# Gated attention's output product and the last pair of MLP groups by seven block products each

## The chip, the cores and the metric

The kernel runs on one core of one Trainium2 chip, as one program. The metric is the device time of one execution in microseconds. A core has a matrix engine (TensorE, PE, with its weight loader PEld), three engines for elementwise work (VectorE or DVE, ScalarE or ACT, GpSimd or POOL), a queue processor that issues the DMAs (SyncE, SP), an on-chip memory (SBUF) and eight banks of 128x512 fp32 in which matmuls accumulate (PSUM).

## The reference

A trunk of two layers on one sequence of 512 tokens with 1024 features. Layer 0 mixes tokens by gated linear attention, layer 1 by stick-breaking attention on keys and values that are projected once. Behind each mixer and each MLP stands a LayerNorm of `ALPHA * h + y`. Cut to the parts that the change touches:

```python
def gla_mixer(x, w_in, w_a2, b_a, norm_g, w_o):
    ...
    o = o * lax.rsqrt(jnp.mean(jnp.square(o), axis=-1, keepdims=True) + RMS_EPS)
    o = o * norm_g.astype(jnp.float32)
    o = o * jax.nn.silu(g.astype(jnp.float32).reshape(B, S, GLA_HEADS, GLA_HEAD_V))
    return o.reshape(B, S, GLA_V).astype(x.dtype) @ w_o

def sq_relu_mlp(x, w_up, w_down):
    h = jax.nn.relu(x @ w_up)
    return (h * h) @ w_down

def reference(...):
    for layer in range(DEPTH):
        ...
        h = layer_norm(DEEPNORM_ALPHA * h + mix, ln_g[layer, 0], ln_b[layer, 0])
        h = layer_norm(DEEPNORM_ALPHA * h + sq_relu_mlp(h, mlp_w_up[layer], mlp_w_down[layer]),
                       ln_g[layer, 1], ln_b[layer, 1])
    return h
```

`gla_w_o` is 1024x1024, `mlp_w_up` 1024x4096, `mlp_w_down` 4096x1024, all fp32.

## The kernel before

**Arithmetic.** fp32 operands are split into a high and a low half in the format fp32r: ScalarE writes `hi` (a copy with rounding), VectorE writes `lo = raw - hi`. A product of two split tiles is three matmuls, hi x hi, hi x lo and lo x hi (`mm3`, L91 to L95). One tile step is 128 tokens, 128 of the contraction and 512 output columns.

**Tiles.** Tokens are four tiles of 128. The residual rows are the four tiles `h` of 128x1024 (class `Rows`): `add` puts a finished PSUM bank into one half of a row (L165 or L167), `stat` takes its statistics (L175), `stats` makes mean and variance from both halves (L179, L181) and on GpSimd the power -1/2 (L183), `centre` subtracts and scales (L187), `affine` applies gain and bias in four pieces of 512 columns (L193). Activations that serve as the stationary or contracted side are kept feature-major in tiles `T` of 128x4x512; PE makes them from rows by 128x128 transposes. `turn_affine` transposes four blocks of a row (L211), applies gain and bias on ScalarE while leaving PSUM (L214) and splits the result (`put`, L98 and L99).

**Weights** come by DMA in pieces of 128x1024 (two contraction tiles of 512 columns, or eight of 128), through 3 buffers `raw`, and are split into 6 buffers each of `hi` and `lo` (L70, L72).

**Gated attention, last part.** For each half n of the 1024 features and each token tile t, `gate` makes the gate product, its Silu and the gated row `os_`; `turn_gated` transposes four blocks of it into `onT`, a split operand. The output product takes `onT` with `gla_w_o`: first the columns 0 to 511 of all four token tiles, 24 matmuls for each, then the columns 512 to 1023 tile by tile inside `finish`. `finish` calls for each tile t: the product of the tile, its `stats`, its `centre`, and then the transposes of tile t-1 (`turn`). So tile t-1 is turned on PE behind the product of tile t. The transposes of the last tile are returned as `late` and run in the middle of the next stage.

**MLP.** Its 4096 hidden features are eight groups of 512. `up(g)` makes a group's product (96 matmuls), then relu (L543, ScalarE) and square (L544, VectorE) into a tile `s2` (three buffers). The groups are taken down in pairs. The pairs (0,1), (2,3) and (4,5) go through `down`: with hidden tokens and weights as 2x2 blocks (256 tokens, a group of 512, 512 columns) it makes the pair's 2x2 result by seven block products instead of eight, each of 24 matmuls of 512 columns (L592), 168 in all. Its operands are sums and differences of the blocks, made on VectorE, of activations (`s1`, `s2`, in place of `a21` and `a12`) and of weights (in place in the 8 buffers `B`), and each is split before use. A bank collects several products; its state is added to a row after each of them. The pair (6,7) goes through `down_last`: 192 matmuls by `mm3`, for columns 0 to 511 first group by group, then for columns 512 to 1023 tile by tile, in layer 0 inside `finish` as above, in layer 1 inside a loop which applies the last norm to each row and sends it out (`norm`, L198 to L204). There the last tile goes in two halves of 256 columns (L649).

**Order.** Each engine runs its own list of instructions in order; the order between engines comes from semaphores on the tiles. The program's text, a scheduler that moves instructions within it, and the number of buffers in each pool set the lists. SyncE issues all weight DMAs in the order of the text as their buffers come free.

## Time and profile before

| | |
|---|---|
| median of 3 runs | 1151.99 us (1151.84 to 1152.28) |
| the profiled execution's own time | 1152.1 us |
| its span | 1150.4 us |
| granted clock of TensorE, mean | 0.998 |
| matmuls with weight load on PE | 5485 |

The span is what the profiler saw from the first to the last instruction; the rest of the profiled execution's time lies around it. In the profile a row of the timeline or of the chain is start and duration in us, engine, line, operation, out<-in by the names of the program, shapes; what is in square brackets is the idle time of the engine ahead of it and what ended that. A window's row is its bounds, its length, busy time and number of instructions of PE, PEld, DVE, ACT and POOL, the granted clock, the DMA engines' busy share and GB/s. Each digit of part 2 below is a fortieth of the span:

```profile
PE   8999999999999999999999999999999999999997
DVE  4576644786877857845834878786958868678556
ACT  4454433543534524623634666654534435346320
```

The gated output product lies at 181.5 to 228 us, the MLP of layer 0 at 235 to 566, its last pair from 520 us on, and the last pair of layer 1 from 1099.4 us to the end.

### The profile page before, as it was taken

What the parts mean: (1) busy time and instruction counts of PE and PEld (TensorE: products, weight loads), DVE (VectorE), ACT (ScalarE), POOL (GpSimd) and SP (SyncE); (2) the same over time, 40 slices, a digit from 0 to 9 for tenths busy, and PEclk for the clock granted to TensorE, in tenths of its full rate; (3) what the DMA queues carried; (4) which work ended last, traced back from release to release, by engine and by line L of the source; (5) the groups of instructions that cost most, each with busy time, mean ns of one, the idle gap of its engine ahead of it and who ended that gap; (6) DMA issues with size and microseconds to landing.
All of it is one profiled execution on the core that took longest, in us unless ns stands there. A gap on an engine that the chain in (4) does not pass through costs nothing.

```text
span 1150.4 us, 14083 instructions
## 1 busy us (share of the span) xinstructions
PE 1133.6 (99%) x5485; PEld 939.9 (82%) x5485; DVE 795.9 (69%) x984; ACT 513.9 (45%) x784; POOL 96.5 (8%) x159
## 2 busy tenths in 40 slices
PE   8999999999999999999999999999999999999997
PEld 6788888898888888888888877778988888888886
DVE  4576644786877857845834878786958868678556
ACT  4454433543534524623634666654534435346320
POOL 1010100000000000000101444340000000000001
PEclk9999999999999999999999999999999999999999
DMA  7441123292360450142244111111732613601402
GB/s 234 125 122 45 53 89 132 79 284 78 110 198 22 148 167 15 37 148 93 72 128 126 58 56 56 57 54 37 248 119 86 203 42 112 198 20 37 135 31 74
DMA packets 86214, 118.71 MB, mean 103 GB/s; under 512 B 11202, under 2 KB 36930, under 8 KB 86148
## 3 DMA queue, kind: packets, MB, share of 16 engines
q1 hardware_dynamic: 86148, 117.81, 32.4%
q8 instruction: 43, 0.70, 0.2%
q14 instruction: 23, 0.19, 0.1%
HBM read 115.70 MB, written 2.10 MB: 102 GB/s over the span
## 4 chain that ended last, share of the span: by engine, by line
PE 83%; DVE 11%; ACT 2%; issue 2%; POOL 1%; DMA 0%; SPq 0%; DVEq 0%; POOLq 0%; ACTq 0%
PE ps L93 20%; PE ps L592 20%; PE ps L94 20%; PE ps L95 20%; DVE r L754 4%; DVE lo L72 2%; ACT wt L769 1%; DVE h L193 1%; DVE ps L746 1%; DVE T L99 1%; DVE qs L729 1%; ACT hi L70 1%; PE ps L121 1%; DVE bst L175 1%; POOL rs L183 1%
## 5 line engine op out<-in xcount | busy, mean ns | idle before, releaser
L72 DVE TENSOR_TENSOR lo<-raw,hi 128x1024 fp32r<-128x1024 f32 x152 | 185.3, 1226 | 156.2 <-ACT hi L70 154.3
L93 PE MATMUL ps<-T,hi 128*128 128x512 f32 (+1 forms) x768 | 288.7, 376 | 0.0
L95 PE MATMUL ps<-T,lo 128*128 128x512 f32 (+1 forms) x768 | 285.5, 372 | 0.0
L94 PE MATMUL ps<-T,hi 128*128 128x512 f32 (+1 forms) x768 | 285.5, 372 | 0.0
L70 ACT ACTIVATE hi<-raw 128x1024 fp32r<-128x1024 f32 x152 | 161.7, 1067 | 238.0 <-PE ps L94 109.5
L592 PE MATMUL ps<-hi,T 128*128 128x512 f32 x672 | 207.9, 389 | 0.0
L93 PE MATMUL ps<-hi,T 128*128 128x512 f32 (+1 forms) x456 | 179.2, 393 | 0.0
L95 PE MATMUL ps<-hi,T 128*128 128x512 f32 (+1 forms) x456 | 176.8, 388 | 0.0
L94 PE MATMUL ps<-lo,T 128*128 128x512 f32 (+1 forms) x456 | 176.6, 387 | 0.0
L95 PEld LDWEIGHTS ps<-T,lo 128*128 128x128 f32 x768 | 144.7, 188 | 25.1
L93 PEld LDWEIGHTS ps<-T,hi 128*128 128x128 f32 x768 | 144.7, 188 | 24.6 <-issue 1.1
L94 PEld LDWEIGHTS ps<-T,hi 128*128 128x128 f32 x768 | 144.8, 189 | 23.4
L592 PEld LDWEIGHTS ps<-hi,T 128*128 128x128 f32 x672 | 126.1, 188 | 26.3
L592 PE MATMUL ps<-lo,T 128*128 128x512 f32 x336 | 130.7, 389 | 0.0
L70 ACT ACTIVATE hi<-B 128x1024 fp32r<-128x1024 f32 x72 | 76.3, 1059 | 109.3 <-PE ps L94 75.3
L72 DVE TENSOR_TENSOR lo<-B,hi 128x1024 fp32r<-128x1024 f32 x72 | 87.5, 1222 | 46.2 <-ACT hi L70 45.8
L95 PEld LDWEIGHTS ps<-hi,T 128*128 128x128 f32 x456 | 85.9, 188 | 17.7 <-DVE T L99 0.3
L93 PEld LDWEIGHTS ps<-hi,T 128*128 128x128 f32 x456 | 86.1, 189 | 17.4 <-issue 1.3
L94 PEld LDWEIGHTS ps<-lo,T 128*128 128x128 f32 x456 | 86.0, 189 | 16.7 <-DVE lo L99 0.3
L183 POOL TENSOR_TENSOR rs<-ve,mhalf 128x1 f32<-128x1 f32 x16 | 12.8, 800 | 784.2 <-DVE ve L181 784.2
L167 DVE TENSOR_TENSOR h<-ps,h 128x512 f32<-128x512 f32 x91 | 62.4, 686 | 20.7 <-PE ps L95 20.5
L592 PEld LDWEIGHTS ps<-lo,T 128*128 128x128 f32 x336 | 63.1, 188 | 12.9
(155 smaller groups left out, 1168.8 us busy)
## 6 DMA issues: line engine op xcount, KB each, us to landing
raw<-in_mlp_w_up_dram SPq DMA_DIRECT2D x64, 512.0 KB, 4.0
B<-in_mlp_w_down_dram SPq DMA_DIRECT2D x48, 512.0 KB, 4.4
raw<-in_mlp_w_down_dram SPq DMA_DIRECT2D x28, 512.0 KB, 3.7
raw<-in_gla_w_in_dram SPq DMA_DIRECT2D x20, 512.0 KB, 3.9
raw<-in_kv_w_dram SPq DMA_DIRECT2D x16, 512.0 KB, 4.1
raw<-in_gla_w_o_dram SPq DMA_DIRECT2D x8, 512.0 KB, 5.1
raw<-in_sb_w_q_dram SPq DMA_DIRECT2D x8, 512.0 KB, 3.8
raw<-in_sb_w_o_dram SPq DMA_DIRECT2D x8, 512.0 KB, 3.6
```

What stands on the lines that cost most here:

```text
L70: nc.scalar.activation(hi, raw, AF.Copy)
L72: nc.vector.tensor_tensor(lo, raw, hi.bitcast(F32), op=ALU.subtract)
L93: nc.tensor.matmul(ps, lhsT=a[0], rhs=b[0], start=first, stop=False)
L94: nc.tensor.matmul(ps, lhsT=a[0], rhs=b[1], start=False, stop=False)
L95: nc.tensor.matmul(ps, lhsT=a[1], rhs=b[0], start=False, stop=last)
L99: keep(nc.vector.tensor_tensor(lo, ps, hi.bitcast(F32), op=ALU.subtract))
L121: nc.tensor.transpose(out=ps[:, 128 * i:128 * i + 128], in_=src[:, 128 * i:128 * i + 128], identity=ident)
L167: nc.vector.tensor_tensor(h, ps, h, op=ALU.add)
L175: nc.vector.bn_stats(out=self.st[:, parts * n + i, :], in_=h)
L183: nc.gpsimd.tensor_tensor(rs, ve, mhalf[:, 0:1], op=ALU.pow)
L592: nc.tensor.matmul(banks[s], lhsT=a(k, s)[x], rhs=b[k][y], start=opens and (k, x, y) == (0, 0, 0), stop=closes and (k, x, y) == (3, 1, 0), ...
L754: nc.vector.tensor_tensor_scan(down, down, begins[kind][:, ::-1], 1.0, op0=ALU.mult, op1=ALU.max)
```

## The change

`down` becomes a generator `seven` outside of the MLP, which takes the two halves of an activation (each 128x4x512 fp32), a function that gives the weight blocks, a pool for the buffers `B`, and the rows. It makes the same seven block products in another order, and adds to a row after each:

- a11 with block b(2), a12 with b(3), s2 with b(2), s1 with b(1): as before, 24 matmuls each for two token tiles;
- a12 (now changed) with the plain block, first for token tile 0, then for token tile 1, with a `yield` behind each: these rows are complete;
- for token tile 2 the products of a21 with b(0) and of a22 with b(3), a `yield`, then both for token tile 3.

The middle pairs run it to its end. The last pair is passed to `finish` (layer 0) or to the loop of the last norm (layer 1), which takes one step for each token tile; `down_last` and `parts` go. In layer 1 (`narrow`) the very last product goes in two halves of 256 columns. The gated output product goes through `seven` too. For that, `turn_gated` writes `onT` as plain fp32 by one copy on ScalarE (L594) in place of a split; the last of these transposes runs behind the first product (`mid`), and the sums s1 and s2 behind it. The pool `heads` is closed earlier, and a pool `gated` with 4 buffers `sg` and 8 buffers `B` stands in its place. `Rows.st`, the tile of a row's statistics, is made at the first `stat`, whichever half comes first.

The core of the diff (the body of `down` that goes is the body of `seven` that is kept, but for the order):

```diff
+    def seven(a1, a2, weights, pool, hs, fresh, norms=False, mid=None, narrow=False):
...
+        def raw(h, k, j):
+            b = pool.tile([P, 1024], F32, tag="B", bufs=8, name=nm("B"))
+            nc.sync.dma_start(out=b.rearrange("p (a b) -> p a b", a=2), in_=weights(k, h, j))
+            return b
...
+            for c in pieces:
+                for k in range(4):
+                    for x, y in ((0, 0), (0, 1), (1, 0)):
+                        nc.tensor.matmul(banks[s][:, c], lhsT=a(k, s)[x], rhs=b[k][y][:, c],
+                                         start=opens and (k, x, y) == (0, 0, 0),
+                                         stop=closes and (k, x, y) == (3, 1, 0), skip_group_check=True)
...
+        if not mid:
+            sums()
+        for b22, b12, b11, b21 in bs:
+            tt(b22, b22, b12, op=ALU.subtract)
+            tt(b12, b12, b11, op=ALU.subtract)
+        product(split_a(a11), split_b(2), ys, True, False, 0, 0)
+        if mid:
+            mid()
+            sums()
+        q12 = split_a(a12)
+        tt(a21, a11, a21, op=ALU.subtract)
+        product(q12, split_b(3), xs, True, True, 0, 0, last=True)
+        tt(a12, a12, s2, op=ALU.subtract)
+        for b22, b12, b11, b21 in bs:
+            tt(b11, b22, b11, op=ALU.add)
+            tt(b21, b21, b11, op=ALU.subtract)
+        product(split_a(s2), split_b(2), ys, False, False, 0, 1)
+        product(split_a(s1), split_b(1), zs, True, False, 1, 1)
+        how = split_a(a12), plain_b(1, 1), zs, False, True, 0, 1
+        for s in range(2):
+            part(s, *how, last=True)
+            yield
+        hows = [(split_a(a21), split_b(0), ys, False, False, 1, 1), (split_a(a22), split_b(3), ys, False, True, 1, 0)]
+        for s in range(2):
+            for how in hows:
+                part(s, *how, last=True)
+            yield
...
-        transpose_into(onT, n, t, os_[t][:, 512 * n:512 * n + 512])
+        ps = bank()
+        for i in range(4):
...
+        nc.scalar.activation(onT[n][:, :, 128 * t:128 * t + 128], ps.rearrange("p (a b) -> p a b", a=4), AF.Copy)
...
-    pcs = pieces_512(gla_w_o[0], 0, 8, 0)
-    for t in range(NT):
-        hs[t].add(0, rows(onT, t, pcs, K8), True, True)
-        if t == 0:
-            turn_gated(3, 1)
+    steps = seven(*onT, lambda k, h, j: block(gla_w_o[0], 512 * k + 256 * h, 512 * j), opp, hs, True, norms=True,
+                  mid=lambda: turn_gated(3, 1))
     hT = Split()
-    pcs = pieces_512(gla_w_o[0], 0, 8, 512)
-    late = finish(lambda t: hs[t].add(1, rows(onT, t, pcs, K8), True, True), vcols, hs, hT, g2)
+    late = finish(lambda t: next(steps), vcols, hs, hT, sgs)
...
-        sqs = [parts(sq[NG - 2]), parts(up(NG - 1))]
-        got = down_last(NG - 2, *sqs)
+        steps = down(NG - 2, norms=True, narrow=l == 1)
+        got = done(lambda t: next(steps), work)
```

**How the lists of the engines move: the start of layer 0's last pair.** ScalarE in the kernel before, around the relu of the last group (L543, tile s2673); T655 is the high half of group 6's activations (s2602), which the first matmuls of the pair take, and each `hi` a piece of weights:

```order
L98 ACTIVATE T655_3968<-s2602_3661 128x512 x4
L70 ACTIVATE hi658_3980<-raw657_3978 128x1024
L70 ACTIVATE hi661_3986<-raw660_3984 128x1024
L70 ACTIVATE hi664_3992<-raw663_3990 128x1024
L70 ACTIVATE hi667_3998<-raw666_3996 128x1024
L70 ACTIVATE hi677_4123<-raw676_4121 128x1024
L70 ACTIVATE hi680_4129<-raw679_4127 128x1024
L70 ACTIVATE hi683_4135<-raw682_4133 128x1024
L70 ACTIVATE hi686_4141<-raw685_4139 128x1024
L70 ACTIVATE hi697_4259<-raw696_4257 128x1024
L543 ACTIVATE s2673_4102<-ps669_4002 128x512
L543 ACTIVATE s2673_4102<-ps670_4003 128x512
```

And VectorE of the changed kernel at the same place, where s2689 is the tile of group 7's squares (L660), s2620 that of group 6, T704 holds the sums s1 and s2 (L329, L330), T705 is the split of a11, T712 the split of a12:

```order
L72 TENSOR_TENSOR lo723_4261<-B698_4149,hi722_4259 128x1024
L660 TENSOR_TENSOR s2689_4128<-ps685_4028,s2689_4128 128x512
L660 TENSOR_TENSOR s2689_4128<-ps686_4029,s2689_4128 128x512
L660 TENSOR_TENSOR s2689_4128<-ps687_4030,s2689_4128 128x512
L72 TENSOR_TENSOR lo725_4265<-B702_4157,hi724_4263 128x1024
L660 TENSOR_TENSOR s2689_4128<-ps688_4031,s2689_4128 128x512
L329 TENSOR_TENSOR T704_4161<-s2620_3697,s2689_4128 128x4x256
L99 TENSOR_TENSOR T705_4168<-s2620_3697,T705_4168 128x4x256
L330 TENSOR_TENSOR T704_4161<-T704_4161,s2620_3697 128x4x256
L99 TENSOR_TENSOR T712_4207<-s2689_4128,T712_4207 128x4x256
L342 TENSOR_TENSOR s2620_3697<-s2620_3697 128x4x256
```

In the kernel before the split of what the first matmuls take (T655) stands ahead of the last group's relu and square; now the split of a11 (T705, of group 6 too) stands behind the four squares and behind the sum s1. On ScalarE the high half of T705 follows the four relus in the same way.

**The end of layer 0's last pair.** VectorE in the changed kernel, from the last addition of row 0 (h300) to the affine of row 1 (h301); lo780 and lo783 are pieces of weights for layer 1's value product, T691 the low half of row 0's first transposed tile:

```order
L168 TENSOR_TENSOR h300_1602<-ps731_4304,h300_1602 128x512
L176 BN_STATS bst718_4233<-h300_1602 128x6
L180 BN_AGGR mv740_4361<-bst718_4233 128x2
L183 TENSOR_SCALAR ve741_4363<-mv740_4361 128x1
L189 TENSOR_SCALAR h300_1602<-h300_1602,mv740_4361,rs742_4365 128x1024
L72 TENSOR_TENSOR lo780_4579<-raw778_4575,hi779_4577 128x1024
L168 TENSOR_TENSOR h301_1603<-ps732_4318,h301_1603 128x512
L72 TENSOR_TENSOR lo783_4585<-raw781_4581,hi782_4583 128x1024
L176 BN_STATS bst720_4249<-h301_1603 128x6
L99 TENSOR_TENSOR T691_4138<-s2746_4389,T690_4137 128x4x128
L180 BN_AGGR mv743_4382<-bst720_4249 128x2
L195 TENSOR_TENSOR h300_1602<-h300_1602,lng816_4857 128x512
```

and PE at that place, with the last matmuls of row 1 (ps732), the transposes of row 0 and row 1 (L213) and the next product (ps710, row 2):

```order
L213 MATMUL ps747_4390<-ident_68,h300_1602 128x128 x4
L213 MATMUL ps749_4402<-ident_68,h300_1602 128x128 x4
L213 MATMUL ps765_4472<-ident_68,h301_1603 128x128 x4
L213 MATMUL ps767_4484<-ident_68,h301_1603 128x128 x3
L306 MATMUL ps710_4179<-hi751_4416,T750_4413 128x512
L306 MATMUL ps710_4179<-lo752_4418,T750_4413 128x512
L213 MATMUL ps767_4484<-ident_68,h301_1603 128x128
L306 MATMUL ps711_4193<-hi751_4416,T750_4413 128x512
L306 MATMUL ps710_4179<-hi751_4416,T750_4413 128x512 x2
```

PE in the kernel before, with the last matmuls of row 1 there (h303, ps718), the transposes of row 0 (h302) and the product of row 2 (ps726):

```order
L94 MATMUL ps718_4323<-lo707_4279,T674_4111 128x512
L95 MATMUL ps718_4323<-hi706_4277,T675_4112 128x512
L211 MATMUL ps723_4358<-ident_68,h302_1607 128x128 x4
L211 MATMUL ps725_4370<-ident_68,h302_1607 128x128 x4
L93 MATMUL ps726_4381<-hi697_4259,T655_3968 128x512
L94 MATMUL ps726_4381<-lo698_4261,T655_3968 128x512
L95 MATMUL ps726_4381<-hi697_4259,T656_3969 128x512
```

Before, the product of the next row stood on PE between the transposes of one row and those of the next; now the transposes of row 1 follow those of row 0 with nothing between them, and the products of row 2 come behind both.

**The gated stage.** ScalarE in the kernel before, where T288 is the second half of the split operand and hi342 and hi345 are weights of the columns 512 to 1023:

```order
L70 ACTIVATE hi339_1778<-raw338_1776 128x1024
L98 ACTIVATE T288_1460<-ps324_1675 128x4x128
L70 ACTIVATE hi342_1784<-raw341_1782 128x1024
L70 ACTIVATE hi345_1790<-raw344_1788 128x1024
L70 ACTIVATE hi377_2009<-raw376_2007 128x1024
```

and in the changed kernel, where T287 is the second half of the plain operand (its columns of token tile 3 come from ps328), hi344 and hi346 are the weights of the second product, T329 is the high half of a12:

```order
L594 ACTIVATE T287_1460<-ps299_1595 128x4x128
L619 ACT_TABLE_LOAD
L70 ACTIVATE hi341_1746<-B318_1634 128x1024
L70 ACTIVATE hi344_1779<-B313_1624 128x1024
L70 ACTIVATE hi346_1783<-B317_1632 128x1024
L594 ACTIVATE T287_1460<-ps328_1682 128x4x128
L98 ACTIVATE T329_1690<-T287_1460 128x4x256
L98 ACTIVATE T338_1739<-T320_1638 128x4x256
```

The copy of the last transposed tile (ps328) has moved behind the weight pieces hi344 and hi346, and the split of a12, which the second product takes, stands behind that copy.

More of the change, by code (lines that the diff above doesn't have):

```diff
@@ L179, in stats @@
             nc.vector.bn_aggr(out=mv, in_=self.st)
+            self.st = None
             ve = small(1, "ve")
@@ L481, in turn_gated, with sgs @@
     def turn_gated(t, n):
-        transpose_into(onT, n, t, os_[t][:, 512 * n:512 * n + 512])
+        ps = bank()
+        for i in range(4):
+            c = slice(128 * i, 128 * i + 128)
+            nc.tensor.transpose(out=ps[:, c], in_=os_[t][:, 512 * n + 128 * i:512 * n + 128 * i + 128], identity=ident)
+        nc.scalar.activation(onT[n][:, :, 128 * t:128 * t + 128], ps.rearrange("p (a b) -> p a b", a=4), AF.Copy)
     pcs = pieces_512(w_in, 0, 8, 2 * QK + D)
     heads[3].scores()
-    onT.grow()
+    sgs = g2
     gate(0, 0, pcs)
     heads[3].outputs()
+    hp.__exit__(None, None, None)
+    op = tc.tile_pool(name="gated", bufs=1, reuse_waits="tile")
+    opp = op.__enter__()
+    def sgs():
+        return opp.tile([P, 512], F32, tag="sg", bufs=4, name=nm("sg"))
+    onT.append(unit(F32))
     for t in (1, 2, 3):
@@ L653, in mlp, with down @@
+        def down(g, **how):
+            return seven(*sq[g:g + 2], lambda k, h, j: block(mlp_w_down[l], 512 * (g + k) + 256 * h, 512 * j), mlp_,
+                         hs, g == 0, **how)
         sq = [up(0), up(1)]
@@ L657, in mlp @@
             sq.append(up(g + 2))
-            down(g, *sq[g:g + 2])
-            if g < NG - 4:
-                sq.append(up(g + 3))
-        sqs = [parts(sq[NG - 2]), parts(up(NG - 1))]
-        got = down_last(NG - 2, *sqs)
+            for _ in down(g):
+                pass
+            sq.append(up(g + 3))
+        steps = down(NG - 2, norms=True, narrow=l == 1)
+        got = done(lambda t: next(steps), work)
         ml.__exit__(None, None, None)
```

153 lines of the change are left out of this document (57 added, 96 removed).

## The prediction

> **What bounds the kernel now.** I read the page first (parts 1 and 2), then the chain that ended last, then the timeline at the joints between stages.
>
> ```profile
> span 1150.4 us, 14083 instructions
> PE 1133.6 (99%) x5485; PEld 939.9 (82%) x5485; DVE 795.9 (69%) x984; ACT 513.9 (45%) x784; POOL 96.5 (8%) x159
> 296.78 38.08 PE ps L592 x168
> 459.98 38.08 PE ps L592 x168
> ```
>
> TensorE (PE) is never idle for long. The last two rows are pieces of the chain: a middle pair of MLP groups runs its 168 matmuls back to back in 38.08 us, so one matmul of 512 columns costs 38.08 / 168 = 0.2267 us of PE's time. PE's number of matmuls is the time of this kernel, as long as nothing starves it.
>
> How near the other engines are to starving it is read by stage. The windows are the gated output product, a middle pair by seven products, and the last pair of layer 0 and of layer 1 (columns: window, length, then busy time and count of PE, PEld, DVE, ACT, POOL, clock, DMA share, GB/s).
>
> ```profile
> 181.50:228.00 46.50, 46.50 (x221) 38.69 (x220) 29.03 (x45) 18.45 (x32) 2.33 (x3) 1.00 0.33 110
> 459.98:498.06 38.08, 38.08 (x170) 31.54 (x169) 31.48 (x38) 21.21 (x23) 0.00 (x0) 1.00 0.22 66
> 519.80:565.90 46.10, 46.10 (x218) 38.43 (x217) 30.05 (x48) 18.41 (x34) 1.93 (x3) 1.00 0.18 58
> 1099.40:1143.00 43.60, 43.60 (x216) 37.05 (x215) 27.23 (x47) 5.58 (x8) 2.74 (x3) 1.00 0.09 31
> ```
>
> The middle pair already keeps VectorE (DVE) busy for 31.48 of 38.08 us, and much of what it needs was made ahead, beside the up products before it.
>
> **What is removed.** Three products of 192 matmuls become 168 each: 3 x 24 x 0.2267 = 16.3 us of PE time, 5.44 us in each stage. That is certain. Everything else is what PE now waits for.
>
> **What is added on DVE.** In each of the three stages the operands must be split and summed: 14 splits of weights (8 before), 7 splits of activations of 128x1024, 8 sums of weights, 4 of activations, 14 additions into the rows (8 before). The price is the step from one start to the next when DVE has no idle time:
>
> ```profile
> 563.82 0.69 DVE L193 TENSOR_TENSOR h<-h,lnb 128x512 f32<-128x512 f32 x1
> 564.42 1.22 DVE L72 TENSOR_TENSOR lo<-raw,hi 128x1024 fp32r<-128x1024 f32 x1
> 565.55 0.69 DVE L99 TENSOR_TENSOR T<-s,T 128x512 fp32r<-128x512 f32 x1
> 566.16 0.68 DVE L167 TENSOR_TENSOR h<-ps,h 128x512 f32<-128x512 f32 x1
> ```
>
> So 0.60 us for 512 columns and 1.13 us for 1024. Per stage that is 33 x 1.13 + 14 x 0.60 = 46 us, and normalization comes on top, beside 38.1 us of matmuls. In a middle pair the surplus lies under the up products on both sides. The last pair has one up product ahead (the weights' sums do go there) and nothing after; what remains is in the order shown above, and I add it up row by row.
>
> **Step 1, the start of a last pair (twice).** The trace of the middle pair shows how the end of an up product falls; call the first block matmul's place, 459.98, t = 0.
>
> ```profile
> 457.98 1.96 ACT L543 ACTIVATE s<-ps 128x512 f32<-128x512 f32 x3 [2.51 <-PE ps L95]
> 459.85 1.06 ACT L70 ACTIVATE hi<-B 128x1024 fp32r<-128x1024 f32 x1
> 460.82 0.57 ACT L543 ACTIVATE s<-ps 128x512 f32<-128x512 f32 x1
> 462.09 0.68 DVE L544 TENSOR_TENSOR s<-ps,s 128x512 f32<-128x512 f32 x1
> ```
>
> The same four rows stand in the new last pair (relu L659, hi, relu, square L660). But there the split of a11 (T705), which the first matmul needs, now stands behind them: ScalarE (ACT) ends the last relu at t + 1.41 and the hi half at t + 2.4; DVE ends the square at t + 2.8, makes the sum s1 (1.13) and only then the lo half, done at t + 5.2. PE can do three matmuls (0.68) with the hi half alone. Stall: 5.2 - 0.7 = **4.5 us**, in layer 0 and in layer 1. The old last pair had split this group before (T655 in the rows of before) and waited for nothing there.
>
> **Step 2, the rows completed one by one, layer 0.** From a row's last addition to PE's transposes:
>
> ```profile
> 1126.64 0.69 DVE L167 TENSOR_TENSOR h<-ps,h 128x512 f32<-128x512 f32 x1 [3.96 <-PE ps L95]
> 1127.36 0.70 DVE L175 BATCH_NORM_STATS2 bst<-h 128x6 f32<-128x512 f32 x1
> 1128.09 0.21 DVE L179 BATCH_NORM_AGGREGATE mv<-bst 128x2 f32<-128x12 f32 x1
> 1128.34 0.15 DVE L181 TENSOR_SCALAR ve<-mv 128x1 f32<-128x1 f32 x1
> ...
> 570.29 0.15 DVE L181 TENSOR_SCALAR ve<-mv 128x1 f32<-128x1 f32 x1
> 570.36 0.68 DVE L193 TENSOR_TENSOR h<-h,lng 128x512 f32<-128x512 f32 x1
> 571.47 0.81 DVE L187 TENSOR_SCALAR h<-h,mv,rs 128x1024 f32<-128x1024 f32 x1 [0.44 <-POOL rs L183]
> 572.34 0.87 PE L211 MATMUL ps<-ident,h 128*128 128x128 f32 x6 [0.84 <-DVE h L187]
> ```
>
> 1.70 to the variance, 1.18 through GpSimd's power to the centring, 0.87 to PE: 3.75 us, and 0.2 for the last matmul to land. Before, 24 matmuls (5.44 us) of the next tile covered that. Now:
> - Row 0 completes with 12 matmuls (2.72 us) of row 1 behind it. DVE's queue reaches its last addition at about t + 29 (15 pieces of 1.13 and 10 of 0.60 after the lo half at t + 5, and half a us of waits), as the matmuls do: 3.95 - 2.72 = 1.2 us of stall.
> - Row 1's transposes stand next on PE, ahead of the products a21 and a22. DVE, from row 0's centring (0.73), does two weight splits (2.27), an addition and a statistic (1.2), a split of row 0's turn (0.6), the aggregate (0.12), an affine (0.6), then variance to transposes (1.18 + 0.87): 7.6 us, of which PE has 0.87 behind it already and fills 0.9 with row 0's eight transposes. Stall 5.8.
> - The lo half of a21 follows row 1's centring by three affine and turn pieces: 0.73 + 3 x 0.60 + 1.22 = 3.8, against 0.87 + 1.5 of PE's transposes and first three matmuls: 1.4.
> - To row 2's centring DVE then needs 4 x 1.13 + 11 x 0.60 + 0.24 = 11.4, then 1.18 + 0.87, together 13.4 from the start of that lo half; PE waits 1.25 of it for the half itself and has 45 matmuls (10.2) for the rest: 2.0. Row 3, behind a value product: 0.35.
>
> Sum for layer 0: 4.5 + 1.2 + 5.8 + 1.4 + 2.0 + 0.35 = 15.25 us, less the 0.84 that PE idles there already (row at 572.34) and less 5.44: **+9.0 us**.
>
> **Step 3, the gated stage.** Its first product runs in time: it needs the first two tiles alone. Call its end e.
>
> ```profile
> 180.00 1.06 ACT L70 ACTIVATE hi<-raw 128x1024 fp32r<-128x1024 f32 x1 [0.29 <-PE ps L95]
> 234.90 0.85 PE L211 MATMUL ps<-ident,h 128*128 128x128 f32 x6 [0.66 <-DVE h L187]
> ```
>
> The first row is a weight split that waits for PE to free its buffer. Two such (hi344, hi346) now stand on ACT ahead of the copy of the last transposed tile, and wait for the first product's buffers: they end at e + 1.0, the copy at 1.6, the hi half of a12 (1.06) at 2.75. PE has four transposes (0.36) and waits 2.4. It can do four matmuls with that half (0.9, to 3.65); DVE makes s1 from the copy (2.7 to 3.85) and then the lo half, at 5.05: 1.4. The rows' ends go as in layer 0 with DVE's list a little different: row 0's addition comes 0.35 late behind a weight split (1.55), row 1's list has one affine less ahead of the variance (5.8 - 0.6 = 5.2), a21's half is the same within 0.2 (1.2), row 2's list has 13 pieces of 0.60 instead of 11 and less is left to PE (2.6); row 3 is covered by 48 matmuls. Sum 14.35, less the 0.94 idle now (0.66 and the issue beside it in the row at 234.90, after a matmul at 233.96), less 5.44: **+8.0 us**.
>
> **Step 4, the tail, layer 1.** The start costs 4.5 and PE then runs through, ending 0.7 us earlier than now. But DVE is behind.
>
> ```profile
> 1098.03 1.37 DVE L544 TENSOR_TENSOR s<-ps,s 128x512 f32<-128x512 f32 x2 [1.94 <-ACT s L543]
> 1143.27 0.42 DVE L649 TENSOR_TENSOR h<-ps,h 128x256 f32<-128x256 f32 x1 [0.32 <-PE ps L95]
> ```
>
> t = 0 is 1098.03 + 1.37 here (as 458.61 stood to 459.98), and the last addition now starts at t + 43.9. In the new order 17 pieces of 1.13 and 10 of 0.60 (25.2) separate the lo half that starts at t + 4 and steps to 5.1 from row 0's last addition, t + 30.4; then the norms of rows 0, 1 and 2 with the additions between them follow with no gap, 5.45 each (0.72 + 0.72 + 0.25 for the statistics, 1.3 + 1.45 for the norm, an addition and a statistic of the next row), so the last addition starts at t + 46.8: **+2.9 us**.
>
> **A cost that one place of this trace shows.** Windows of the kernel's beginning and of one gap in its middle (clock: the third number from the end):
>
> ```profile
> 4.00:6.00 2.00, 0.76 (x4) 0.36 (x2) 0.57 (x1) 1.11 (x2) 0.06 (x2) 1.00 0.89 214
> 6.00:8.00 2.00, 0.89 (x5) 0.58 (x5) 1.28 (x3) 1.15 (x2) 0.00 (x0) 1.00 0.91 330
> 8.00:10.00 2.00, 1.81 (x7) 1.62 (x8) 0.83 (x3) 0.73 (x3) 0.00 (x0) 0.52 1.05 404
> 10.00:12.00 2.00, 2.00 (x7) 1.63 (x6) 1.26 (x2) 0.46 (x1) 0.00 (x0) 0.62 1.11 352
> ...
> 757.00:760.50 3.50, 1.84 (x13) 1.43 (x12) 2.50 (x4) 1.96 (x7) 1.19 (x2) 1.00 0.00 0
> ```
>
> After 4 us in which PE was busy for 1.65 (41%), the granted clock fell to half for some 3.4 us: (1 - 0.52) x 2 + (1 - 0.62) x 2 = 1.7 us lost. With 1.84 of 3.5 us busy (53%) it held. The stalls of step 1 (0.7 busy in 5.2 us) and of row 1 (5.8 and 5.2, with only transposes around) are emptier than either. Five places at 0 to 1.7 us bound this by 0 and 8.5. I take 5, since part of it falls where DVE is the later one anyway.
> The Trainium skill, "TensorE: Matmul & The Clock Gate", section "HAM oscillation — how this bites in real kernels", says that a matmul engine idle for a window of about 3.4 us is set back to half its clock. The trace agrees at its beginning; the rule alone would make each of the five a full loss, and the sum 1180 instead of 1177.
>
> **The sum**, against the profiled execution's own 1152.1 us (median of the runs shown: 1151.99, so no shift): 1152.1 + 9.0 + 8.0 + 2.9 + 5 = **1177 us**, slower by 2.2%.
>
> **The rivals.**
> - *The stalls, but the clock holds*: 1152.1 + 19.9 = 1172. For it: the row at 757 us, where half an empty window cost nothing. Chance 0.35; the forecast with the clock 0.40.
> - *The count decides* (faster): DVE's rows overlap more than their order says, so that PE stalls for less than 16.3 us in all three stages together; it decides where DVE's 46 us per stage fall under 38 + what it does ahead. With no stall 1135.8; with only the starts (2 x 4.5 + 3.8) it is 1148.6. For it: 99% busy now and middle pairs of the same form with no gap. Against it: steps 1 and 2 are single-engine queues, in which nothing can be passed. Chance 0.11, and 0.03 for within the noise.
> - *Weights late as well*: eight more buffers of 512 KB are wanted beside one up product instead of three. The 31 to 110 GB/s of the windows above speak against (404 in the row at 8 us); with 3 us per stage more it is 1186. Chance 0.11.
>
> **How the numbers follow.** Likeliest 1177. The bounds of the clock's cost give 1172 to 1180; an error of a quarter in the 34 us of stalls is 8.5 us each way: 1163 to 1189. That leaves out the 0.11 of the faster case and little else. A measurement of this kernel can tell some 0.2% from no change: slower 0.86, within 0.03, faster 0.11.
>
> **What would show it.** PE idle for about 4.5 us, with three matmuls inside, at the start of both last pairs; a gap of over 5 us before the second group of transposes at the end of the gated stage and of layer 0; DVE near 90% in those stretches; a granted clock below 1 right after; the last addition later by 3 us against the last up product. If PE shows 99% again and those gaps are under 1 us, steps 1 and 2 are wrong. If the gaps are there and the clock stays at 1, only the last term falls.

## The result, and the profile after

The changed kernel takes 1183.07 us (median of 4 runs, 1181.55 to 1184.67) beside 1152.13 for the kernel before: a ratio of 1.0269, 95% interval 1.0251 to 1.0287. The profiled execution took 1182.95 us, with a span of 1181.0. The page of the changed kernel, first lines and the clock:

```profile
span 1181.0 us, 14039 instructions
PE 1137.2 (96%) x5401; PEld 934.0 (79%) x5401; DVE 877.0 (74%) x1053; ACT 546.5 (46%) x807; POOL 96.2 (8%) x159
...
PEclk9999998899999999998899999999999999999988
```

PE has 84 instructions less and is 44 us less than the span, where it was 17 less. The clock has three notches, at the gated stage, at the end of layer 0's MLP and at the end.

**Where the time went.** The relus of a hidden group and the Silu of a gate product exist in both kernels, so their starts mark the same places. Timeline of ScalarE, the kernel before (last Silu; first relu of groups 0 and 7 of layer 0, and of 0 and 7 of layer 1):

```profile
181.36 0.60 ACT L474 ACTIVATE g<-ps 128x512 f32<-128x512 f32 x1 [0.30 <-PE ps L95]
252.25 1.58 ACT L543 ACTIVATE s<-ps 128x512 f32<-128x512 f32 x3 [0.92 <-PE ps L95]
517.82 1.28 ACT L543 ACTIVATE s<-ps 128x512 f32<-128x512 f32 x2 [2.57 <-PE ps L95]
831.77 1.08 ACT L543 ACTIVATE s<-ps 128x512 f32<-128x512 f32 x2 [0.86 <-PE ps L95]
1097.40 0.60 ACT L543 ACTIVATE s<-ps 128x512 f32<-128x512 f32 x1 [2.57 <-PE ps L95]
```

and the changed kernel:

```profile
181.97 0.60 ACT L582 ACTIVATE sg<-ps 128x512 f32<-128x512 f32 x1 [0.31 <-PE ps L95]
263.23 1.09 ACT L659 ACTIVATE s<-ps 128x512 f32<-128x512 f32 x2 [0.91 <-PE ps L95]
529.60 0.60 ACT L659 ACTIVATE s<-ps 128x512 f32<-128x512 f32 x1 [2.52 <-PE ps L95]
855.05 0.60 ACT L659 ACTIVATE s<-ps 128x512 f32<-128x512 f32 x1 [0.86 <-PE ps L95]
1121.46 0.60 ACT L659 ACTIVATE s<-ps 128x512 f32<-128x512 f32 x1 [2.52 <-PE ps L95]
```

The differences of neighbouring rows: 0.6 us ahead of the gated stage (where nothing changed), **+10.4 in the gated stage**, +0.8 through the middle pairs of layer 0, **+11.5 in layer 0's last pair**, +0.8 through those of layer 1, and to the end of the span **+6.5 in the tail**. Together 30.6.

What PE waits for in the three stages, by the view of waits (in all, times, longest; two answers of the changed kernel, the gated stage and layer 0's end), where the kernel before has a single wait of 0.7 us in the one and a single wait of 0.8 us in the other:

```profile
PE ps L213 <- DVE h L189: 6.0, 2, 4.9
PE ps L306 <- ACT T L98: 2.2, 1, 2.2
PE ps L306 <- DVE h L168: 1.3, 1, 1.3
PE ps L306 <- DVE T L99: 0.4, 1, 0.4
```

```profile
PE ps L213 <- DVE h L189: 6.3, 2, 5.6
PE ps L306 <- ACT T L98: 2.4, 1, 2.4
PE ps L306 <- DVE T L99: 1.9, 1, 1.9
PE ps L306 <- DVE h L168: 1.0, 1, 1.0
```

and in the tail:

```profile
PE ps L306 <- DVE h L311: 2.8, 1, 2.8
PE ps L306 <- ACT T L98: 2.4, 1, 2.4
PE ps L306 <- DVE T L99: 1.2, 1, 1.2
PE ps L306 <- DVE h L168: 0.8, 1, 0.8
```

L213 waiting for L189 is the transposes waiting for a row's centring, L98 and L99 are the halves of an activation split. L168 is an addition into a row: in layer 0 the matmul that waits for it is the first of row 3's second product, which goes on in the bank that this addition reads, and row 2's transposes behind it wait for nothing (timeline of PE):

```profile
585.42 0.50 PE L306 MATMUL ps<-hi,T 128*128 128x512 f32 x1 [1.01 <-DVE h L168]
...
588.41 1.10 PE L213 MATMUL ps<-ident,h 128*128 128x128 f32 x8
```

The first row of the tail is new: L311 is the addition of one half of the very last product, and PE waits for it before the other half.

The clock behind the two gaps of layer 0 (windows):

```profile
535.00:542.00 7.00, 5.17 (x12) 4.11 (x13) 6.82 (x7) 3.13 (x4) 0.00 (x0) 0.52 0.00 0
569.00:576.00 7.00, 2.50 (x11) 2.21 (x11) 6.54 (x12) 5.69 (x13) 0.54 (x1) 0.53 0.46 149
```

7 us at 0.52 are 6.7 us at half speed. In windows of half a microsecond each of the five such stretches ahead of the tail's end measures 6.83 us in this execution (two in the gated stage, two in layer 0, one at the start of the tail), twice the 3.41 at the beginning of the kernel before.

### The profile page after: what moved, and what is told of

Read it like the earlier page. It is cut to its first block, busy times and chain, and to the rows that moved or that the text cites. A ratio compares the mean times of both kernels' runs of the same rounds, so it can differ in the third digit from the quotient of the medians.

```text
span 1181.0 us, 14039 instructions
## 1 busy us (share of the span) xinstructions
PE 1137.2 (96%) x5401; PEld 934.0 (79%) x5401; DVE 877.0 (74%) x1053; ACT 546.5 (46%) x807; POOL 96.2 (8%) x159
## 4 chain that ended last, share of the span: by engine, by line
PE 78%; DVE 15%; ACT 3%; issue 2%; POOL 1%; DMA 0%; SPq 0%; DVEq 0%; POOLq 0%; ACTq 0%
PE ps L306 26%; PE ps L93 16%; PE ps L94 16%; PE ps L95 16%; DVE r L769 4%; DVE lo L72 3%; ACT wt L784 1%; DVE T L99 1%; DVE h L168 1%; ACT hi L70 1%; DVE bst L176 1%; DVE ps L761 1%; DVE qs L744 1%; PE ps L213 1%; POOL rs L185 1%
## 5 line engine op out<-in xcount | busy, mean ns | idle before, releaser
L306 PE MATMUL ps<-hi,T 128*128 128x512 f32 (+1 forms) x1016 | 326.7, 399 | 16.4 <-ACT T L98 7.0
L306 PEld LDWEIGHTS ps<-hi,T 128*128 128x128 f32 x1016 | 195.5, 194 | 64.6 <-ACT T L98 8.1
L306 PE MATMUL ps<-lo,T 128*128 128x512 f32 (+1 forms) x508 | 201.4, 396 | 0.0
L70 ACT ACTIVATE hi<-B 128x1024 fp32r<-128x1024 f32 x108 | 114.5, 1060 | 171.7 <-PE ps L94 99.4
L72 DVE TENSOR_TENSOR lo<-B,hi 128x1024 fp32r<-128x1024 f32 x108 | 131.1, 1222 | 64.1 <-ACT hi L70 63.5
L306 PEld LDWEIGHTS ps<-lo,T 128*128 128x128 f32 x508 | 98.4, 194 | 19.6
L94 PE MATMUL ps<-lo,T 128*128 128x512 f32 x256 | 100.8, 394 | 0.0
L168 DVE TENSOR_TENSOR h<-ps,h 128x512 f32<-128x512 f32 x109 | 74.6, 686 | 13.6 <-PE ps L306 9.5
L769 DVE TENSOR_TENSOR_SCAN r<-r,begin 128x512 f32<-128x512 f32 x40 | 66.2, 1663 | 0.2
L660 DVE TENSOR_TENSOR s<-ps,s 128x512 f32<-128x512 f32 x64 | 43.3, 688 | 19.4 <-ACT s L659 19.4
L770 POOL TENSOR_TENSOR w<-w,r 128x512 f32<-128x512 f32 x40 | 51.4, 1285 | 75.7 <-DVE r L769 60.5
```

What stands on the lines that cost most here:

```text
L70: nc.scalar.activation(hi, raw, AF.Copy)
L72: nc.vector.tensor_tensor(lo, raw, hi.bitcast(F32), op=ALU.subtract)
L94: nc.tensor.matmul(ps, lhsT=a[0], rhs=b[1], start=False, stop=False)
L168: nc.vector.tensor_tensor(h, ps, h, op=ALU.add)
L306: nc.tensor.matmul(banks[s][:, c], lhsT=a(k, s)[x], rhs=b[k][y][:, c], start=opens and (k, x, y) == (0, 0, 0), stop=closes and (k, x, y) = ...
L660: nc.vector.tensor_tensor(s2[:, f, :], pss[f], s2[:, f, :], op=ALU.mult)
```

## The experiments

Two theories go through all expectations. **A**: each wait costs by itself, from its place in the engines' orders, and a long one costs half speed besides (the prediction's way of adding). **B**: VectorE's amount of work in a stage is the bound, and PE meets its backlog wherever it waits. The stages of all kernels against the kernel before, read from the same rows as above:

| kernel | median us | gated | layer 0's last pair | tail |
|---|---|---|---|---|
| changed kernel | 1183.07 | +10.4 | +11.5 | +6.5 |
| e1 a11 split early | 1176.14 | +9.3 | +9.4 | +3.9 |
| e2 filler matmuls | 1175.28 | +9.4 | +9.9 | +2.6 |
| e3 a21, b(0) split ahead | 1179.12 | +9.6 | +9.5 | +7.1 |
| e4 both halves first | 1180.54 | +11.5 | +11.8 | +3.8 |
| e5 lo halves on GpSimd | 1185.11 | +13.1 | +11.6 | +6.3 |
| e6 = e1 + e3 + e4 | 1169.06 | +7.5 | +5.9 | +1.0 |
| e7 = e6 + e5 | 1176.91 | +9.3 | +9.4 | +4.4 |
| e8 = e7 + more off VectorE | 1188.37 | +8.9 | +12.3 | +13.5 |
| e9 = e6 + square on ScalarE | 1171.95 | +9.2 | +7.0 | +1.8 |
| e10 layer 1's last pair alone | 1152.85 | 0.0 | +0.1 | +0.8 |
| e11 = e10 + square on ScalarE | 1154.11 | 0.0 | +0.1 | +2.7 |
| e12 = e10 + more work ahead | 1148.96 | 0.0 | 0.0 | -3.1 |

The gated stage is the same instruction for instruction in the changed kernel, e1, e2 and e4, and PE's gaps in it agree to 0.02 us where the clock is up; still it differs by 2.2 us. Windows of its first gap, the changed kernel and e1 (which runs 1.5 us earlier there):

```profile
190.00:198.00 8.00, 7.17 (x17) 5.17 (x18) 6.69 (x7) 2.39 (x3) 0.00 (x0) 0.57 0.11 43
```

```profile
190.00:198.00 8.00, 6.76 (x24) 5.45 (x24) 7.35 (x9) 3.72 (x4) 0.00 (x0) 0.79 0.00 0
```

8 us at 0.57 hold 6.8 us of half speed, 8 at 0.79 hold 3.4. So the gated stage is read to about 1 us either way only, the stages of e10 to e12 that are as before to 0.1. In layer 0 the changed kernel, e1, e3, e4 and e5 all spend some 13.7 us at half speed, so there they can be compared more closely; e6 spends half of that.

**e1.**

```diff
...
-        product(split_a(a11), split_b(2), ys, True, False, 0, 0)
+        product(q11 or split_a(a11), split_b(2), ys, True, False, 0, 0)
...
+            q11 = split_u(sq[NG - 2][:, :, 0:256]) if g == NG - 4 else None
             sq.append(up(g + 3))
```

> Both last pairs split a11 (of group 6) ahead of the last up product, as the kernel before did. Theory A (the prediction's: every wait of PE read off the engines' orders costs by itself, and a long one costs a stretch at half clock besides): in layer 0 the start's two gaps of 2.79 and 2.25 us shrink to a step each (-4.6) and the 13 steps of 0.427 us behind them to 0.227 (-2.6), in layer 1 only the split's own 1.1 us and VectorE's idle 0.7 go, since VectorE sets that end: about -9, 1174 us. Theory B (VectorE's amount of work in a stage is the bound, and PE meets its backlog wherever it waits): in layer 0 VectorE idles for only 3.0 us between the start and row 0's statistics, so at most 1.1 + 3.0 come back there, and 1.1 to 1.8 in layer 1: -2 to -6, 1177 to 1181 us, with PE's gaps later in the pair grown.

Measured: 1176.14 us, between the two forecasts, but 2.6 of the 7.2 us by which the profiled executions differ lie in the gated stage and ahead of it, where nothing changed. Layer 0 is 2.1 us shorter, in B's range and far from A's 7.2; the tail is 2.7 us shorter, more than either had (1.8). The gap at the start is gone, the clock stays up there, and PE comes to row 0's transposes 6.2 us sooner within the pair (29.9 from the last group's relu to the last matmul ahead of them, 36.1 in the changed kernel). There it waits (timeline of PE, e1, layer 0):

```profile
561.06 1.97 PE L213 MATMUL ps<-ident,h 128*128 128x128 f32 x8 [3.71 <-DVE h L189]
564.21 1.97 PE L213 MATMUL ps<-ident,h 128*128 128x128 f32 x8 [1.18 <-DVE h L189]
569.22 0.80 PE L311 MATMUL ps<-hi,T 128*128 128x512 f32 x1 [3.04 <-ACT T L98]
```

Row 0's wait grew from 0.8 to 3.7, row 1's fell from 5.6 to 1.2, and a21's split, which hardly showed in the changed kernel, now costs 3.0.

**e2.**

```diff
+        b2 = split_b(2)
+        if fill:
+            w = bank()
+            for i in range(fill):
+                tc.keep_in_program_order(nc.tensor.matmul(w, lhsT=b2[0][0][:, 0:128], rhs=b2[0][0], start=True,
+                                                          stop=True))
...
```

> Eleven matmuls (2.5 us) whose result nobody reads stand ahead of the first block product of both last pairs, in PE's wait there. Nothing that VectorE or ScalarE do changes. Theory A: PE's longest idle stretch at the start falls from 2.8 to under 2.3 us, the granted clock stays at 1.0 there, 13 steps in layer 0 take 0.227 us again: -2.6, and 0 to -0.7 in layer 1, 1180 us. Theory B: the clock holds too, but only the 1.2 us that VectorE waited for slow matmuls come back in layer 0: -1.2 or less, 1182 us. If the clock falls all the same, idleness is not what lowers it.

The clock holds at both starts (windows of e2, layer 0 and layer 1):

```profile
533.00:540.00 7.00, 6.10 (x26) 4.39 (x26) 7.00 (x7) 3.80 (x5) 0.00 (x0) 1.00 0.00 0
1124.00:1131.00 7.00, 6.33 (x27) 4.92 (x28) 7.00 (x8) 3.80 (x5) 0.00 (x0) 1.00 0.00 0
```

Idleness lowers it, then. 1175.28 us lies under both forecasts, and the sizes, -1.7 in layer 0 and -3.9 in the tail, don't separate A from B: contrary to what was expected, the fillers made the scheduler move VectorE's list too. In the tail the first half's addition now stands ahead of row 2's norm, which takes away most of the wait that e4 is about.

**e3.**

```diff
+        q21 = split_a(a21), split_b(0)
         for s in range(2):
             part(s, *how, last=True)
             yield
-        hows = [(split_a(a21), split_b(0), ys, False, False, 1, 1), (split_a(a22), split_b(3), ys, False, True, 1, 0)]
+        hows = [(*q21, ys, False, False, 1, 1), (split_a(a22), split_b(3), ys, False, True, 1, 0)]
```

> In all uses of the seven products, the splits of a21 and of b(0) are written ahead of the two products that complete rows 0 and 1; the orders then have the products of row 2 and row 3 with a21 between the transposes of row 0 and those of row 1, and row 0's affine pieces behind row 1's centring. Theory A: the stall ahead of row 1's transposes (5.2 us in the gated stage, 5.8 in layer 0) falls to about 1, the one for a21's lo half (1.2 and 1.4) to 0, row 0's grows by 1.1, with less half clock behind: -4 to -6 in each of the two stages, 0 in the tail, about 1173 us. Theory B: VectorE has the same pieces, only the four affine pieces (2.4 us) come behind the stage: -2 or so in each, 1179 us.

Row 1's wait is gone (0.34 in layer 0), as A has it; the stage got only 2.0 shorter, as B has it, because row 2's now is 3.7 (timeline of PE, e3, layer 0: transposes of rows 0, 1 and 2):

```profile
565.33 1.09 PE L213 MATMUL ps<-ident,h 128*128 128x128 f32 x8 [0.53 <-DVE h L189]
572.01 1.09 PE L213 MATMUL ps<-ident,h 128*128 128x128 f32 x8 [0.34 <-DVE h L189]
...
583.30 1.97 PE L213 MATMUL ps<-ident,h 128*128 128x128 f32 x8 [3.68 <-DVE h L189]
```

The tail, with PE's order unchanged, moved by +0.6; the gated stage moved by less than its own spread.

**e4.**

```diff
             for c in pieces:
                 for k in range(4):
...
-                if len(pieces) > 1:
+            if len(pieces) > 1:
+                for c in pieces:
```

> Layer 1's very last product makes both halves of its 256 columns before either is added to the row. If PE's 3.07 us gap between the halves is the second half's wait for the first half's addition out of the same bank, the second half now runs at once, and the last addition starts right behind the first, at t + 47.4 in place of t + 50.5: -3.0, 1180 us. If PE waits there for something else (the row's norm work on VectorE, an operand), nothing moves: 1183 us.

The tail is 2.8 us shorter, and the two additions stand side by side (VectorE, e4):

```profile
1169.12 1.54 DVE L205 SCALAR_TENSOR_TENSOR h<-h,rs,lnb 128x512 f32<-128x512 f32 x3
1170.57 0.75 DVE L312 TENSOR_TENSOR h<-ps,h 128x256 f32<-128x256 f32 x2
```

So the wait was for the bank: in the order of the changed kernel PE's second half stood until the addition had read the first half out of the same bank, and where both halves are written first there is no such wait.

**e5.**

```diff
-                hi, lo = split_tile(bs[h][i], 2)
+                hi, lo = split_tile(bs[h][i], 2, eng)
...
+        (eng or nc.vector).tensor_tensor(lo, raw, hi.bitcast(F32), op=ALU.subtract)
```

> The four lo halves of b(0) and of the second b(3) are made on GpSimd in the gated stage and in both last pairs, all else as in the changed kernel: 4.5 us less on VectorE in each. They stand ahead of row 0's last addition; between row 0's centring and row 1's, VectorE's list stays as it was. Theory A (each wait by itself, from its place in the lists): in layer 0 row 0's gap cannot fall under 3.95 - 2.72 = 1.2 and row 1's of 5.8 stays: 0; gated -0.4; the tail, which VectorE ends, -4.5: about -5, 1178 us. Theory B (VectorE's amount): -3 to -4.5 in each of the three: -9 to -13, 1170 to 1174 us.

In layer 0 the stage moved by 0.05 us: A's 0, not B's -3 to -4.5. VectorE, with four pieces less, waits for PE between the additions (VectorE, e5, layer 0):

```profile
559.70 0.69 DVE L168 TENSOR_TENSOR h<-ps,h 128x512 f32<-128x512 f32 x1 [2.03 <-PE ps L306]
562.42 0.69 DVE L168 TENSOR_TENSOR h<-ps,h 128x512 f32<-128x512 f32 x1 [2.03 <-PE ps L306]
565.14 0.69 DVE L168 TENSOR_TENSOR h<-ps,h 128x512 f32<-128x512 f32 x1 [2.03 <-PE ps L306]
```

So up to row 0 the changed kernel is paced by PE, delayed at the start, and not by VectorE. Both theories had the tail at -4.5 (it is -0.2), and nobody had the gated stage at +2.7. There, the four pieces took GpSimd 10.99 us, 2.7 each, where VectorE needs 1.13, and PE's waits for the rows' centrings rose from 6.0 to 9.3 us, while its 1.3 for an addition fell away. So e5 took 4.5 us off VectorE's list but was no clean trial of its amount outside layer 0.

**e6.** The edits of e1, e3 and e4 together.

> The three edits together that were tried one by one: a11 split ahead of the last up product, the splits of a21 and b(0) ahead of the rows' last products, both halves of the last product ahead of their additions. Their measured stages added up: layer 0 -2.1 - 2.0, gated -0.5, tail -2.65 - 2.8, in all -10: 1173 us. Theory A, by which a removed wait comes back in full when nothing else stands in its way: layer 0 -7.2 - 5.8, gated -5, tail -5: -23, 1160 us. Theory B: VectorE now works with hardly a gap from the start on, and what the single edits left over is all there is: -10 to -13, 1170 to 1173 us.

1169.06, 14.0 us less than the changed kernel: somewhat more than the parts added and than B's range (10 to 13), far from A's 23. The 4 us beyond the parts lie in the gated stage (2.4) and in layer 0 (1.5); in each of them e6 spends 6.8 us less at half speed, which is up to 3.4 us of PE's time, so the clock alone can account for them. Two windows of layer 0, from the start to row 0's centring and from there to the end of the stage:

```profile
530.00:562.40 32.40, 31.84 (x145) 25.91 (x143) 32.11 (x40) 16.93 (x19) 1.16 (x2) 1.00 0.11 33
562.40:585.00 22.60, 15.46 (x59) 11.83 (x58) 20.50 (x32) 15.51 (x34) 2.83 (x6) 0.85 0.47 140
```

Up to row 0 VectorE now has hardly an idle moment (32.11 of 32.40 us), and PE is as full. What PE still waits for comes behind, where VectorE is busy for 20.5 of 22.6 us: there B fits, though 2.6 us of PE's waits are for ScalarE.

**e7 and e8.** e7 is e6 with e5's edit; e8 adds this:

```diff
-                    nc.vector.tensor_tensor(self.h[:, c], self.h[:, c], v[:, c], op=op)
+                    tc.keep_in_program_order(nc.gpsimd.tensor_tensor(self.h[:, c], self.h[:, c], v[:, c], op=op))
...
+            nc.scalar.activation(self.h, self.h, AF.Identity, bias=nb, scale=self.rs)
```

> e6 and the four lo halves on GpSimd as in e5. Theory A: in layer 0 and in the gated stage VectorE's pieces ahead of row 0 cost nothing that PE sees, so 0 there against e6, -4.5 in the tail. Theory B: with the waits of the lists out of the way, VectorE's amount is all that is left, and each of the three stages gets 4 to 4.5 us shorter than in e6: -12 to -13 against e6, near 1160 us.

> e7, and more taken off VectorE: the affine pieces of the rows behind every first norm and behind layer 0's last (16 of 0.60 us for each set of rows) go to GpSimd, behind the powers that the next rows wait for; of the last norm, rows 0 and 1 go through ScalarE (scale and shift, one pass) and GpSimd (gain and bias), 5.5 us less for VectorE in the tail. Theory A: nothing that PE waits for moves but the tail: -3 to -5 against e7. Theory B: a few affine pieces less ahead of the rows' centrings, -2 to -3 in the gated stage and in layer 0, -5 in the tail: -9 to -11 against e7, near 1150 us, about where the kernel before stands.

Both failed: e7 is 7.9 us slower than e6, e8 19.3. VectorE of e7 in layer 0, with GpSimd's row of the same time:

```profile
548.61 0.68 DVE L168 TENSOR_TENSOR h<-ps,h 128x512 f32<-128x512 f32 x1
549.21 2.82 DVE L72 TENSOR_TENSOR lo<-raw,hi 128x1024 fp32r<-128x1024 f32 x1
551.95 0.68 DVE L168 TENSOR_TENSOR h<-ps,h 128x512 f32<-128x512 f32 x1
552.55 2.83 DVE L72 TENSOR_TENSOR lo<-raw,hi 128x1024 fp32r<-128x1024 f32 x1
555.30 3.39 DVE L99 TENSOR_TENSOR T<-s,T 128x1024 fp32r<-128x1024 f32 x1
```

```profile
547.72 13.20 POOL L72 TENSOR_TENSOR lo<-B,hi 128x1024 fp32r<-128x1024 f32 x4 [308.94 <-ACT hi L70]
```

A piece of 1.22 takes VectorE 2.82 to 3.39 while GpSimd runs, and GpSimd's take 3.3. The three pieces shown cost 5.4 us more, which is more than the four that were taken away (4.5). VectorE's busy time did not fall at all (877.3 us of the whole execution, 874.0 in e6), so e7 says nothing against B. In e8's tail the power for row 1 also stands behind row 0's gain and bias on GpSimd (5.0 us).

**e9.**

```diff
+                if g == NG - 1:
+                    nc.scalar.activation(s2[:, f, :], s2[:, f, :], AF.Square)
...
```

> e6, and in the last up product of both layers ScalarE also makes the square (a second pass of 0.5 us over each of the four tiles) that VectorE made: 2.4 us less on VectorE behind the start of both last pairs, where e6 left it without a gap of over 0.7 us; 2 us more on ScalarE ahead of the second half of b(1)'s split. Theory B (with the lists' waits gone, VectorE's amount is the bound): -2.4 in layer 0 and -2.4 in the tail, less up to 1.5 each for the later weight split: -2 to -5 against e6, about 1165.5 us. Theory A (waits by their place): PE's gap at the start grows from 0.95 to about 2.5 us in both and nothing else moves: +1.5 to +3, 1171 us.

A's side, though not by its size: +2.9 by the medians, but 1.7 of it in the gated stage, where all lists are as in e6; +1.2 in layer 0 and +0.8 in the tail. PE's gap at the start grew from 0.95 to 2.01 us, as A has it (2.5). VectorE had nothing to do in the time it was given (e9, layer 0):

```profile
532.74 1.23 DVE L72 TENSOR_TENSOR lo<-B,hi 128x1024 fp32r<-128x1024 f32 x1 [6.00 <-PE ps L311]
```

All its next pieces need the last group or ScalarE's half of a split, and ScalarE is busy with the squares: the half that this piece needs ends there at 532.71, although the view puts the wait down to PE.

**e10, e11.** The kernel before, with e6's form in layer 1's last pair alone; e11 with the square on ScalarE.

> The kernel before, with the seven products for one place alone, layer 1's last pair, in the form of e6 (a11 split ahead, a21 and b(0) split ahead, both halves ahead of their additions); the gated product, the middle pairs and layer 0's last pair are as before. If the stages do not touch each other, this is the tail of e6 by itself: +1.0 against the kernel before, 1152.5 us. If the seven products are a loss in the tail only for what the earlier stages left behind, 5.4 us of PE come back: 1147 us.

> e10 with the last group's square on ScalarE. Theory B: VectorE's 2.4 us less, less up to 1.5 for the later weight split: -1 to -2.4 against e10, 1150 to 1151.5 us, which would be under both kernels. Theory A: +0.7 to +1.5 against e10, 1153.5 us.

e10: 1152.85 us beside 1151.74, ratio 1.0014 (1.0005 to 1.0023); the tail is +0.8 where e6 had +1.0. So the loss in the tail does not come from the earlier stages. e11 is 1.3 us above e10 by the medians (ratio 1.0022, 1.0013 to 1.0031), A's side again: PE's gap at the start grew from 0.94 to 2.02 us.

**e12.** Instead of giving work to a slower engine, this moves it to an earlier time:

```diff
+        q11 = split_a(a11)
+        tt(a21, a11, a21, op=ALU.subtract)
+        q21 = split_a(a21)
+        bh, bl = unit(F32R), unit(F32R)
...
+            put(bh[:, c, :], bl[:, c, :], v(bs[h][0]))
+        a2 = yield
...
+        tt(s2, a22, a21, op=ALU.subtract)
+        tt(s1, s2, a11, op=ALU.add)
```

> e10, and more of the work of layer 1's last pair that needs group 6 and weights alone is made beside the last up product, in activation buffers that are free then: a21's difference and split, b(0)'s split, 4 pieces of 1.13 us; s2 is a22 less that difference, s1 is s2 plus a11. The splits that e11 could not spare came from ScalarE's chain; these have no producer in the last group. In e10 VectorE has no idle time from the start to its last addition, and 3.0 + 1.9 us or so in the up product ahead. If the amount behind the start sets the tail: -4.5, PE's gaps of 2.40 and 1.96 near the end shrink to nothing, 1148.3 us, under both kernels. If VectorE's pieces ahead hold up the last up product's own splits instead: PE gaps there, and 1152 to 1155 us.

1148.96 us beside 1152.04, ratio 0.9968 (0.9957 to 0.9979): faster than both kernels. The tail is 3.1 us shorter than before and 3.9 shorter than in e10, of the 4.5 expected. Of PE's waits from the start to the last product one is left (view of waits, then the window of that stretch, e12):

```profile
PE ps L310 <- DVE h L168: 0.8, 1, 0.8
```

```profile
1099.40:1141.00 41.60, 38.65 (x180) 31.77 (x179) 41.02 (x63) 12.62 (x13) 2.74 (x3) 1.00 0.10 36
```

VectorE still is busy for 41.0 of 41.6 us and goes on without a gap to the last norm, so it sets this tail even now.

## Why the prediction was right, and where it was off

The forecast was 1177 us (1163 to 1189), slower; measured 1183.07. The mechanism held: 16.3 us of matmuls went, and waits for VectorE and ScalarE took their place at the joints named.

- **The starts** (4.5 in both last pairs): 2.79 + 2.25 in place of two steps of 0.227, 4.6 in layer 0, with three matmuls inside; 2.79 + 1.81 in layer 1.
- **The rows of layer 0** (1.2, 5.8, 1.4, 2.0, 0.35): 0.8, 5.6, nearly none, 1.0, 0.6. **The gated stage** (2.4, 1.4, 1.55, 5.2, 1.2, 2.6): 2.2, 0.4, 1.1, 4.9, none, 1.3. The long ones are within 0.3, and the places are right but for one: the 2.0 and the 2.6 were forecast for row 2's centring, and the 1.0 and 1.3 measured are PE's wait for an addition out of a bank (L168), which the prediction does not have. The small ones were too large by some 6.5 us in all; most lie where PE runs at half speed, which would leave VectorE time, but that this is the reason was not tried.
- **The clock** is the term that was mis-sized the other way: five places at 0 to 1.7 us, 5 taken. The stretch at the kernel's beginning, 3.41 us, was taken for the length of all. Those of the changed kernel are 6.83 us, so up to 3.4 us of PE's time each. The gated stage and layer 0 came out at +10.4 and +11.5, where +8.0 and +9.0 stood without the clock. With the measured waits in place of the forecast ones these two would be +3.5 and +6.3, which leaves 6.9 and 5.2 us for the clock (by subtraction): 12 in two stages, above the prediction's bound of 8.5 for all five places. By the Trainium skill, "TensorE: Matmul & The Clock Gate", section "What's actually happening", the monitor's window of 3413 ns is free-running and does not start with the kernel. The trace agrees: behind the gated stage's first gap the same orders give 3.41 us in e1 and 6.83 in the changed kernel. What the prediction took for an agreement with an idle window is none: at the kernel's beginning PE's longest idle time was 1.3 us, and the clock fell all the same.
- **The tail** (+2.9, measured +6.5) failed in one step: "PE then runs through". The addition that was forecast as the last one starts at t + 46.9 (forecast: 46.8), but it was the first half's; PE's second half stood behind it, and its addition started 3.4 us later. Without that wait the tail is 2.8 us shorter (e4).
- **Middle pairs**, costed at nothing, took 1.6 us in six: the next up product's first matmuls now stand among the pair's last, with three longer steps there, 0.2 us in each pair of layer 0; that leaves some of it open.
- **The rivals.** Clock or no clock: it fell, and e2 shows by what. Weights late: none of the waits of PE, VectorE or ScalarE in the three stages is put down to a DMA. The count decides: PE's waits in the three stages are some 29 us, far over 16.3.

That the sum came within 6 us is luck in part: in the gated stage and in layer 0 the waits were 7 us too large and the clock 7 us too small, and what is left is the tail (3.6), the middle pairs (1.6) and 0.6 ahead of the gated stage.

What the prediction did not see is how the waits hang together. It added them up; but a wait taken away does not return its length (e1: 2.1 for the 7.2 that stood there), and work taken off VectorE returned nothing in layer 0 (e5: 0.05 for 4.5). At every joint the later of two lists counts. In the changed kernel VectorE idles for 3.0 us between the start of layer 0's last pair and row 0, since PE is late by more; so the start's wait is worth no more than those 3 us and the 1.1 of the split itself, and VectorE's amount nothing. Once the lists are untangled, VectorE has no idle time left in the tail (e10), and there its amount is the price: e12 gets 3.9 us for 4.5 moved ahead. Why fewer products still lose 5.9 and 7.5 us in layer 0 and in the gated stage of e6 stays open. PE waits there for 7.8 and 9.2 us, of which 2.6 and 4.4 are for ScalarE's halves of splits, so VectorE's amount is not all of it; e12's edit was not tried there.

## What to carry to other kernels

A product with fewer block products buys matmul time with vector work, and paid here only where another product's time lies around it in which that work is done; at the end of a stage, count both lists from the last operand on and take the later one at each joint. What can be made from early operands alone should be made before the last producer runs, in whatever buffers are free there. A faster or slower helper engine, or a single wait removed, moves the time only as far as the other list has slack.

## What the runs showed of the hardware that was not expected

- **Half speed comes in whole windows.** Every stretch at half clock inside the kernels measured 3.41 us or a multiple (6.83, in e1 also 13.65), not always the same behind equal gaps. It needs no empty window: in layer 0 of the changed kernel the clock fell though three matmuls had run between two idle times of 2.4 and 1.9 us, shorter than 3.41 each.
- **VectorE and GpSimd hold each other up.** In e7 a subtraction with both operands in SBUF took VectorE 2.82 to 3.39 us beside GpSimd's and 1.22 alone; an addition with one operand in PSUM took 0.68 in both. The Trainium skill, "SBUF — State Buffer", section "SBUF: two separate sides", has a port pair that one of the two engines holds for a whole instruction, against VectorE's instructions with two SBUF inputs where GpSimd's reads SBUF. The trace of e7 agrees, the PSUM rows included.
